# Squares' products between the next operand's products, the state's copy taken from PSUM, nine merge tiles, and an earlier reordering of the past

## The chip, the core and the metric

The kernel runs on one core of one Trainium2 chip. That core has a matrix engine (TensorE, PE in the profile, with its weight loads as PEld), a vector engine (VectorE, DVE), a scalar engine (ScalarE, ACT), a general engine (GpSimd, POOL), and a sync engine (SP) that here issues most of the transfers between the chip's memory (HBM, "dram" in names) and the core's two memories: SBUF, which holds operands, and PSUM, into which TensorE adds its products. PSUM is used here as eight banks, named pa, pb, pc, pd, pe, mm, mf and so on after the tags of their tiles. The metric is the device time of one execution, in microseconds (us), as the median of several runs.

## The reference

One layer of a hybrid encoder. A normalised input h of 1152 rows (1024 of a prompt, and 8 x 16 of samples) by 1024 is multiplied by one combined matrix; its columns feed three things: forgetting attention ("fox", 8 heads of 64), a gated delta rule ("gdn", 8 heads of 64), and two gates.

```python
h   = RMSNorm_pre(x)
z   = h @ W_in          # fox q,k,v,forget logits | gdn qkv,a,b,out-gate | merge gates A,B
yA  = P_fox(FoX(h))     # exp-decayed causal attention, prompt and sample with a cached past
yB  = P_gdn(GDN(h))     # short causal conv, l2-normalised q and k, gated DeltaNet
x  += RMSNorm_post(W_out(sigmoid(gA)*yA + sigmoid(gB)*yB))
x  += RMSNorm_post(W_down relu(W_up RMSNorm_pre(x))^2)
```

For this change two pieces matter. `l2norm` divides each row of q and k by the root of the sum of its 64 squares. And the delta rule walks over the rows in chunks of 64 with a 64 x 64 state per head:

```python
v_new = u - w @ state
o     = (q * exp(gc)) @ state + ((q @ k.T) * decay) @ v_new
state = state * exp(g_last) + (k * exp(g_last - gc)).T @ v_new
```

## The kernel before

Every large product runs in three passes of 32-bit operands that were split into a rounded part and a rest (hi x hi, lo x hi, hi x lo): `mm3` (L158) issues them, so nearly every big product of the profile has line 158. In the front half each is 128 x 128 weights against 384 columns, a third of the 1152 rows ("a chunk", c = 0, 1, 2); one operand of 128 columns takes 8 x 3 = 24 of them for each chunk. "The big products" below are these.

The program has these stages, by time in the profiled execution: norm, transposes and logits to about 60 us; the delta rule to about 700; fox attention to about 977; the merge of the two with their gates to about 1110; then the output projection and the two MLP products to the end.

**The delta rule's stage** works on four pairs of heads, p = 0 to 3. For a pair, `gdn_in` makes three operands (q, k, v; i = 0, 1, 2) with `gemm_t` into the banks mm, copies them out of PSUM (`ev`), and passes each through the short convolution. For q and k `gdn_squares` squares the operand on ScalarE (L455) and adds the squares over a head's 64 rows by nine small products of 128 x 128 against two columns of ones (L457; each appears as two passes in the trace, so 18 for one operand, 144 in all), into one bank pa; VectorE scales them (L458). `gdn_norms` turns the result into rows in HBM (transposition L660, then stores), and `gdn_systems` fetches these rows back spread over the partitions and multiplies k by them on GpSimd (L482), q on VectorE, and so on, to the small products L520. An inverse of each chunk's triangle follows, then the chain over the chunks. It is this chain that walks with the state S: for each chunk u and pair of heads, L619 multiplies by the state, L620 (VectorE) makes the right side R, L621 multiplies it by the inverse, L623 takes vn out of PSUM, L626 makes the update, L629 makes the new state S on VectorE out of the old one and the PSUM bank, and L633 makes the output out of qa and xs; xs holds a copy of the state in its lower half (L618, one head on VectorE and one on ScalarE, each 64 x 64) and vn in its upper half (L625).

**Fills.** Big products that nothing waits for soon (fox's q, k, v and the merge's gates; tile mf, spilled to HBM through gst) are issued at a low priority, and the scheduler, which writes out one order for each engine from a model of durations when the program is built, lays them where it expects TensorE to wait. There are 2232 of them. They run out at some point, and where, the scheduler decides.

**Fox** begins with the cached past's forget values (`fox_past`, L951 to L953): two GpSimd copies put the columns in another order (q, b, h in place of b, q, h), and a transposition follows. **The merge** loads the outputs of both halves from HBM (`load`, L1167, tiles orw of 128 x 384), splits them, and multiplies for each of eight j by the two projections' weights (raw_..._w_proj_fox and raw_..._w_proj_gdn, split into whi and wlo); the result times the gate goes into a tile mt (L1192), and the sum of both is split into mhi and mlo, which take the place of hhi and hlo in SBUF, the operands of the fills. orw and mt share seven buffers of one tag; two more (wor) receive rows of W_out.

SP issues its transfers strictly in the order written out, so one that waits holds up all behind it; the same holds of every engine's instructions.

## Time and profile before

| | |
|---|---|
| median of 3 runs | 1936.88 us (1934.66 to 1941.57) |
| the profiled execution | 1936.41 us, span 1934.7 us |
| TensorE busy | 1869.5 us, 97% |
| VectorE, ScalarE, GpSimd busy | 1281.3, 996.8, 231.3 us |
| mean granted TensorE clock | 0.987 |
| squares' products L457 | 144, at 74.2 to 465.5 us |
| state's copy L618 on VectorE | 60, at 228.2 to 657.9 us |

The span runs from the first to the last instruction; the 1.7 us beside it lie around the program. A matmul's busy time overlaps its successor's, so what a product costs TensorE is the distance between two starts, not its duration. Idle time "before" an instruction is put down to the instruction that released it. The granted clock is 1 at full speed; a stretch with about 0.5 is one in which TensorE ran at half of it.

### The profile page before, as it was taken

How to read it: one execution, taken by the hardware profiler on the slowest of the kernel's cores; microseconds unless marked ns; L12 is line 12 of the kernel's file. 1: busy time of each engine (PE TensorE's matmuls, PEld its weight loads, DVE VectorE, ACT ScalarE, POOL GpSimd, SP SyncE). 2: the span in 40 equal slices, each digit the busy share in tenths (PEclk: the TensorE clock that was granted, in tenths of full speed). 3: DMA queues.
4: the chain of work that ended last, by engine and by line, in shares of the span. 5: the costliest groups of instructions: out<-in, count | busy, mean ns of one | idle time of the engine just before them, and what ended most of it. 6: DMA issues, size and time to landing. Idle time of an engine off the chain costs nothing. (4 is left out here: it accounts for less than half of the span.)

```text
span 1934.7 us, 31970 instructions
## 1 busy us (share of the span) xinstructions
PE 1869.5 (97%) x11036; PEld 1695.0 (88%) x11036; DVE 1281.3 (66%) x3077; ACT 996.8 (52%) x2373; POOL 231.3 (12%) x348
## 2 busy tenths in 40 slices
PE   7999999999999999999999999999999999999998
PEld 6989989889889888787889988999999998888886
DVE  7457487587664457766654455886667764559697
ACT  6433374474564666666554444555544554345553
POOL 2141332331521110000002200000000000000000
PEclk9989998999999999999999999999999999999999
DMA  7142413323335264434264462234444469846573
GB/s 217 38 104 66 114 43 99 95 68 90 89 85 162 81 192 142 131 113 121 67 211 136 130 210 93 59 115 138 131 137 135 143 188 298 281 150 182 149 263 135
DMA packets 292693, 261.35 MB, mean 135 GB/s; under 512 B 68742, under 2 KB 246910, under 8 KB 292531
## 3 DMA queue, kind: packets, MB, share of 16 engines
q1 hardware_dynamic: 252486, 225.10, 39.5%
q10 hardware_dynamic: 40044, 34.21, 5.4%
q8 instruction: 87, 1.43, 0.3%
q14 instruction: 76, 0.61, 0.1%
HBM read 186.48 MB, written 72.75 MB: 134 GB/s over the span
## 5 line engine op out<-in xcount | busy, mean ns | idle before, releaser
L158 PE MATMUL mf<-hhi,whi 128*128 128x384 f32 x744 | 262.2, 352 | 1.8 <-ACT gst L219 1.8
L158 PE MATMUL mf<-hlo,whi 128*128 128x384 f32 x744 | 262.3, 353 | 0.0
L158 PE MATMUL mf<-hhi,wlo 128*128 128x384 f32 x744 | 261.2, 351 | 0.0
L158 PE MATMUL mm<-th,wh 128*128 128x320 f32 (+1 forms) x896 | 177.9, 294 | 0.0
L158 PE MATMUL mm<-bh,ah 128*128 128x512 f32 x436 | 169.7, 389 | 0.7 <-DVE y L1633 0.7
L158 PE MATMUL mm<-bh,al 128*128 128x512 f32 x436 | 169.7, 389 | 0.0
L158 PE MATMUL mm<-bl,ah 128*128 128x512 f32 x436 | 169.6, 389 | 0.0
L334 ACT CAST ah<-ar 128x512 fp32r<-128x512 f32 x107 | 66.4, 622 | 153.8 <-PE mm L158 102.2
L158 PEld LDWEIGHTS mf<-hhi,whi 128*128 128x128 f32 x744 | 141.5, 190 | 3.1 <-ACT gst L219 2.3
L158 PEld LDWEIGHTS mm<-th,wh 128*128 128x128 f32 x896 | 143.5, 188 | 0.0
L158 PEld LDWEIGHTS mf<-hhi,wlo 128*128 128x128 f32 x744 | 141.7, 191 | 0.3
L158 PEld LDWEIGHTS mf<-hlo,whi 128*128 128x128 f32 x744 | 141.3, 190 | 0.5
L158 PE MATMUL mm<-th,wl 128*128 128x256 f32 x448 | 132.2, 295 | 0.0
L1397 DVE TENSOR_TENSOR s<-mm,s 128x256 f32<-128x256 f32 (+1 forms) x196 | 84.4, 454 | 65.7 <-PE mm L158 53.9
L335 DVE TENSOR_TENSOR al<-ar,ah 128x512 fp32r<-128x512 f32 x107 | 73.6, 689 | 73.8 <-ACT ah L334 73.0
L335 DVE TENSOR_TENSOR wlo<-raw,whi 128x512 fp32r<-128x512 f32 x110 | 78.2, 715 | 65.3 <-ACT whi L334 63.7
L158 PE MATMUL mm<-hhi,whi 128*128 128x384 f32 x288 | 106.5, 370 | 1.6 <-ACT X L395 1.6
L334 ACT CAST whi<-raw 128x512 fp32r<-128x512 f32 x110 | 67.7, 620 | 67.5 <-PE mf L158 28.8
L158 PE MATMUL mm<-hhi,wlo 128*128 128x384 f32 x288 | 102.4, 356 | 0.0
L158 PE MATMUL mm<-hlo,whi 128*128 128x384 f32 x288 | 102.3, 355 | 0.0
L158 PE MATMUL mm<-mhi,wl 128*128 128x256 f32 (+1 forms) x336 | 99.1, 295 | 0.0
L158 PE MATMUL mm<-mhi,wh 128*128 128x256 f32 (+1 forms) x336 | 98.8, 294 | 0.0
(542 smaller groups left out, 4951.9 us busy)
## 6 DMA issues: line engine op xcount, KB each, us to landing
ar<-ua_d SPq DMA_DIRECT2D x124, 256.0 KB
raw<-in_w_in_dram SPq DMA_DIRECT2D x86, 256.0 KB
br<-in_w_down_dram SPq DMA_DIRECT2D x78, 256.0 KB
wr<-in_w_up_dram SPq DMA_DIRECT2D x56, 256.0 KB
ua_d<-s SPq DMA_DIRECT2D x112, 128.0 KB
ua_d<-s ACTq DMA_DIRECT2D x84, 128.0 KB
gate_d<-gst ACTq DMA_DIRECT2D x48, 192.0 KB
ga<-gate_d SPq DMA_DIRECT2D x48, 192.0 KB
```

The source lines that it names most:

```text
L158: T.matmul(out, a, b, start=first and i == 0, stop=last and i == n - 1)
L334: A.copy(h, raw)
L335: V.tensor_tensor(l, raw, f(h), ALU.subtract)
L1397: V.tensor_tensor(r, o, x, ALU.add)
```

## The change

Four edits. **Squares:** `gdn_squares` yields after each of its nine products; `gdn_in` hands the generator to the next operand's `gemm_t`, which, in its last chunk (c = 2), takes one square's product after every three big ones, and what is left at the end. **State's copy:** VectorE's half of xs is no longer copied from S, but made by the same operation as S, from the old state and the PSUM bank, as a 64 x 64 piece (`state`); ScalarE's half is copied from S as before. **Merge tiles:** orw and mt have nine buffers, wor has one. **Past:** the columns are put in order by GpSimd at p = 2 of the delta rule's stage, into a tile of its own, clq.

```diff
--- before.py
+++ after.py
@@ -155,7 +155,8 @@
     def mm3(out, pairs, first=True, last=True):
         n = len(pairs)
         for i, (a, b) in enumerate(pairs):
-            T.matmul(out, a, b, start=first and i == 0, stop=last and i == n - 1)
+            mm = T.matmul(out, a, b, start=first and i == 0, stop=last and i == n - 1)
+        return mm
 
 
     phs = ctx.enter_context(ExitStack())
@@ -348,21 +349,28 @@
                 lo += [l[:, i] for i in range(4)]
         return hi, lo
 
-    def gemm_t(w, xhi, xlo, kt, evac, tag=("mm", 1), prio=1):
+    def gemm_t(w, xhi, xlo, kt, evac, tag=("mm", 1), prio=1, between=iter(())):
 
         whi, wlo = w
         for c in range(3):
             cs = slice(c * CH, (c + 1) * CH)
             acc = pt(*tag)
-            mm3(acc[:, :CH], [pr for k in range(kt) for pr in (
-                (whi[k], tk(xhi, k, c)), (whi[k], tk(xlo, k, c)), (wlo[k], tk(xhi, k, c)))])
+            for k in range(kt):
+                mm = mm3(acc[:, :CH], [(whi[k], tk(xhi, k, c)), (whi[k], tk(xlo, k, c)), (wlo[k], tk(xhi, k, c))],
+                         k == 0, k == kt - 1)
+                if c == 2:
+                    with tc.issue_after(mm.ins):
+                        next(between, None)
             with tc.high_priority(prio):
                 evac(c, acc[:, :CH])
+        for _ in between:
+            pass
 
 
     fox_d = dr.tile([NP_, P, NT], F32, name="fox_d")
     gdn_d = dr.tile([NP_, P, NT], F32, name="gdn_d")
     cl = cb.tile([P, 2, 64], F32, name="cl")
+    clq = cb.tile([P, P], F32, name="clq")
     ngc = cb.tile([P, 1], F32, name="ngc")
     for h in range(2):
         S.dma_start(ngc[64 * h:64 * h + 64], gdn_norm_g[0].unsqueeze(1))
@@ -384,6 +392,7 @@
 
         xt = []
         nv = big(gp, "nv", 2, [P, 3, 36])
+        sq = iter(())
         for i in range(3):
             x = big(gp, "X", XB, [P, XW])
             xv = x[:, 3 + NPR:].rearrange("p (b t) -> p b t", b=NB)
@@ -397,10 +406,10 @@
                     A.copy(x[:, 3 + 2 * CH:3 + NPR], acc[:, 0:256])
                     A.copy(xv[:, :, 3:19], acc[:, 256:384].rearrange("p (b t) -> p b t", b=NB))
             gemm_t(weights(halves(win, W_G + 512 * i + p * P), "w", HI),
-                   hhi, hlo, KT, ev)
+                   hhi, hlo, KT, ev, between=sq)
             xt.append(gdn_conv(gp, p, i, x))
             if i < 2:
-                gdn_squares(gp, i, xt[i], nv)
+                sq = gdn_squares(gp, i, xt[i], nv)
             next(lg, None)
         return *xt, nv
 
@@ -455,6 +464,7 @@
         A.activation(sq, a, AF.Square)
         for t in range(NTT):
             T.matmul(nps[:, t:t + NTT + 1:NTT], sq[:, t * P:(t + 1) * P], ones2, start=True, stop=True)
+            yield
         V.tensor_scalar(nv[:, 0, 2 * NTT * j:2 * NTT * (j + 1)], nps[:, :2 * NTT], 0.25, 0.25 * EPS, ALU.mult, ALU.add)
 
     def gdn_norms(gp, p, qs, ks, vs, nv):
@@ -614,8 +624,8 @@
                     rr = R[:, i]
                     xs = big(gp, "xs", 2, [P, 2, C])
                     if u:
-                        for h in range(2):
-                            (A.copy if h else V.tensor_copy)(xs[0:64, h], st_[64 * h:64 * h + 64])
+                        state(xs[0:64, 0], 0, 64)
+                        A.copy(xs[0:64, 1], st_[64:128])
                         T.matmul(pu[:, 0:C], kbd[:, i], st_, start=True, stop=True)
                         V.scalar_tensor_tensor(rr, pu[:, 0:C], cols[:, 3, u:u + 1], rr, ALU.mult, ALU.subtract)
                     T.matmul(pu[:, C:2 * C], ybd[:, i], rr, start=True, stop=True)
@@ -625,10 +635,14 @@
                         A.copy(xs[64:128, h], vn[64 * h:64 * h + 64])
                     T.matmul(pu[:, 2 * C:3 * C], kd[:, i], vn, start=True, stop=True)
                     st0, st_ = st_, big(gp, "S", 2, [P, C])
-                    if u:
-                        V.scalar_tensor_tensor(st_, st0, gam[:, u:u + 1], pu[:, 2 * C:3 * C], ALU.mult, ALU.add)
-                    else:
-                        V.tensor_copy(st_, pu[:, 2 * C:3 * C])
+
+                    def state(dst, r0, r1, st0=st0, pu=pu, u=u):
+
+                        if u:
+                            V.scalar_tensor_tensor(dst, st0[r0:r1], gam[r0:r1, u:u + 1], pu[r0:r1, 2 * C:3 * C], ALU.mult, ALU.add)
+                        else:
+                            V.tensor_copy(dst, pu[r0:r1, 2 * C:3 * C])
+                    state(st_, 0, P)
                     k0 = 0 if u else 64
                     T.matmul(po[:, i * P:(i + 1) * P], xs[k0:].rearrange("p h c -> p (h c)"),
                              qa[k0:, u].rearrange("p h c -> p (h c)"), start=True, stop=True)
@@ -925,6 +939,10 @@
                 lf_out(gp)
             if p == 2:
                 conv_out(gp)
+
+                for k in range(2):
+                    G.tensor_copy(clq[:, 64 * k:64 * k + 64].rearrange("p (q b h) -> p q b h", q=NP_, b=NB),
+                                  cl[:, k].rearrange("p (b q h) -> p q b h", b=NB, q=NP_))
             if p == 1:
                 for k in range(2):
                     S.dma_start(cl[:, k].rearrange("p (b h) -> p b h", b=NB),
@@ -945,12 +963,7 @@
     def fox_past(fp):
 
         ct = mmt()
-        cq = fp.tile([P, 4 * P], F32, tag="sp3", name=nm("past"))[:, :P]
-
-        for k in range(2):
-            G.tensor_copy(cq[:, 64 * k:64 * k + 64].rearrange("p (q b h) -> p q b h", q=NP_, b=NB),
-                          cl[:, k].rearrange("p (b q h) -> p q b h", b=NB, q=NP_))
-        T.transpose(ct[:, 0:P], cq, ident)
+        T.transpose(ct[:, 0:P], clq, ident)
         fl, on = (fp.tile([P, n * P], F32, tag=f"sp{n - 1}", name=nm("past"))[:64, :PAST + TS] for n in (6, 7))
         G.memset(on, 1.0)
         V.tensor_copy(fl[:, 0:P], ct[0:64, 0:P])
@@ -1163,7 +1176,7 @@
         olo = op.tile([P, 8, NT], F32R, name="olo")
         def load(k, c):
             cs = slice(c * CH, (c + 1) * CH)
-            orw = op.tile([P, CH], F32, tag="mt", bufs=7, name=nm("orw"))
+            orw = op.tile([P, CH], F32, tag="mt", bufs=9, name=nm("orw"))
             S.dma_start(orw, fox_d[k, :, cs] if k < 4 else gdn_d[k - 4, :, cs])
             split(orw, ohi[:, k, cs], olo[:, k, cs])
 
@@ -1174,14 +1187,14 @@
                         load(k, c)
         for j in range(KT):
             if j == 4:
-                w2 = [wo_part(oqa, 0, 0, WK, oqa, "wor", 2)]
+                w2 = [wo_part(oqa, 0, 0, WK, oqa, "wor", 1)]
             js = slice(j * P, (j + 1) * P)
             whi, wlo = weights([w_pf[0][:, js], w_pg[0][:, js]], "w", 200)
             mt = {}
 
             for c, i in [(c, i) for i in (1, 0) for c in range(3)] if j == 0 else [(c, i) for c in range(3) for i in (1, 0)]:
                 cs = slice(c * CH, (c + 1) * CH)
-                mt[c, i] = op.tile([P, CH], F32, tag="mt", bufs=7, name=nm("mt"))
+                mt[c, i] = op.tile([P, CH], F32, tag="mt", bufs=9, name=nm("mt"))
                 ga = op.tile([P, CH], F32, tag="ga", bufs=GAB, name=nm("ga"))
                 with tc.high_priority(200):
                     S.dma_start(ga, gate_d[i, j, :, cs])
```

The first place is TensorE in the delta rule's stage, the first pair, where the squares of q lay in one piece between products of the next operand (mm). Before:

```order
L158 MATMUL mm_3775<-hhi,whi_3739 128x384
L158 MATMUL mm_3775<-hlo,whi_3739 128x384
L158 MATMUL mm_3775<-hhi,wlo_3740 128x384
L457 MATMUL pa_3698<-ones_534,y_3699 128x2 x9
L158 MATMUL mm_3775<-hhi,whi_3739 128x384
L158 MATMUL mm_3775<-hlo,whi_3739 128x384
L158 MATMUL mm_3775<-hhi,wlo_3740 128x384
```

Now, in that operand's last chunk (mm_3789 is its bank):

```order
L158 MATMUL mm_3789<-hhi,whi_3727 128x384
L158 MATMUL mm_3789<-hlo,whi_3727 128x384
L158 MATMUL mm_3789<-hhi,wlo_3728 128x384
L466 MATMUL pa_3793<-ones_534,y_3794 128x2
L158 MATMUL mm_3789<-hhi,whi_3727 128x384
L158 MATMUL mm_3789<-hlo,whi_3727 128x384
L158 MATMUL mm_3789<-hhi,wlo_3728 128x384
L466 MATMUL pa_3793<-ones_534,y_3794 128x2
```

The nine small products (18 passes) no longer follow each other: there are three big ones between each of them, and the last two stand together at the chunk's end, about 42 big products later than the piece stood.

The second place is VectorE in the first steps of the chain. Before, the copy of S follows the operation that made S:

```order
L623 TENSOR_SCALAR vn_4926<-pb_4919 128x64
L643 TENSOR_SCALAR nv_3587<-pd_4899 128x2
L629 SCALAR_TENSOR_TENSOR S_4931<-S_4892,gam_4088,pb_4919 128x64
L618 COPY xs_4935<-S_4931 64x64
L490 TENSOR_TENSOR y_4720<-ks_4429,y_4699 128x576
L620 SCALAR_TENSOR_TENSOR R_4907<-pd_4934,cols_4064,R_4907 128x64
L490 TENSOR_TENSOR y_4720<-ks_4429,y_4699 128x576
L623 TENSOR_SCALAR vn_4941<-pd_4934 128x64
```

Now:

```order
L633 TENSOR_SCALAR vn_4927<-pb_4920 128x64
L500 TENSOR_TENSOR y_4721<-ks_4430,y_4700 128x576
L642 SCALAR_TENSOR_TENSOR S_4932<-S_4893,gam_4089,pb_4920 128x64
L642 SCALAR_TENSOR_TENSOR xs_4936<-S_4893,gam_4089,pb_4920 64x64
L500 TENSOR_TENSOR y_4721<-ks_4430,y_4700 128x576
L630 SCALAR_TENSOR_TENSOR R_4908<-pd_4935,cols_4065,R_4908 128x64
L496 TENSOR_TENSOR qs_4307<-qs_4307,y_4716 128x576
L633 TENSOR_SCALAR vn_4942<-pd_4935 128x64
L611 TENSOR_SCALAR kd_608<-pe_5013,tm 64x64
L496 TENSOR_TENSOR qs_4307<-qs_4307,y_4716 128x576
```

The copy has become a second operation on the PSUM bank (pd, pb); the chain's own operations stand in the same order, and those of the next systems (L490, now L500, and L487, now L496) are still laid between them.

The third place is TensorE after fox's last value product (L1035, now L1048). Before, 79 fills stand behind it, then the merge's first products, with single fills (mf) among them:

```order
L158 MATMUL mf_3531<-hlo,whi_3493 128x384
L158 MATMUL mf_3531<-hhi,wlo_3494 128x384
L158 MATMUL mf_3531<-hhi,whi_3499 128x384
L158 MATMUL pb_11337<-ohi,whi_11329 128x384
L158 MATMUL pb_11337<-olo,whi_11329 128x384
L158 MATMUL pc_11355<-ohi,whi_11329 128x384
L158 MATMUL pc_11355<-olo,whi_11329 128x384
L158 MATMUL mf_3531<-hlo,whi_3499 128x384
L158 MATMUL pb_11337<-ohi,wlo_11330 128x384
L158 MATMUL pb_11337<-ohi,whi_11329 128x384
```

Now 30 fills stand behind it, and then the merge begins, with fox's half (whi_11323):

```order
L158 MATMUL mf_3560<-hhi,whi_3500 128x384
L158 MATMUL mf_3560<-hlo,whi_3500 128x384
L158 MATMUL mf_3560<-hhi,wlo_3501 128x384
L158 MATMUL pe_11391<-ohi,whi_11323 128x384
L158 MATMUL pe_11391<-olo,whi_11323 128x384
L158 MATMUL pe_11391<-ohi,wlo_11324 128x384
```

The other 84 of the 114 fills that stood behind fox's last product (the last 34 of them behind some 220 merge products) now stand earlier, most of them in the delta rule's stage. On SP, at the same place, the second weight of the merge now follows the last of the 24 loads; before it stood behind the eighth:

```order
L1167 DMA orw_11249<-gdn_d 128x384
L1167 DMA orw_11253<-gdn_d 128x384
L343 DMA raw_11327<-in_w_proj_gdn_dram 128x4x128
L1167 DMA orw_11257<-gdn_d 128x384
L1167 DMA orw_11261<-gdn_d 128x384
```

```order
L1180 DMA orw_11309<-fox_d 128x384
L1180 DMA orw_11313<-fox_d 128x384
L1180 DMA orw_11317<-fox_d 128x384
L344 DMA raw_11327<-in_w_proj_gdn_dram 128x4x128
L1200 DMA ga_11352<-gate_d 128x384
```

The load of the weight raw_11327 has moved past 16 loads of orw.

## The prediction

> **What bounds the kernel now.** I read the page first, then the clock in windows, then TensorE's waits.
>
> ```profile
> PE 1869.5 (97%) x11036; PEld 1695.0 (88%) x11036; DVE 1281.3 (66%) x3077; ACT 996.8 (52%) x2373; POOL 231.3 (12%) x348
> ```
>
> TensorE is busy for 97% of the span, and no other engine is near it. So only three things shorten the run: fewer passes (the change keeps every big product), waits of TensorE, and stretches in which its clock is granted at half. Next, the windows around the stretches in which the page's row of the granted clock falls (the columns are start and end, length, PE busy and instructions, granted clock, DMA share, GB/s):
>
> ```profile
> 91.40:94.80 3.40, 3.40 (x29) 1.00 0.02 5
> 94.80:101.70 6.90, 6.90 (x27) 0.51 0.15 38
> 296.20:299.60 3.40, 3.40 (x29) 1.00 0.03 7
> 299.60:306.50 6.90, 6.90 (x26) 0.51 0.17 38
> 323.50:326.90 3.40, 2.49 (x19) 1.00 0.54 146
> 326.90:333.80 6.90, 6.90 (x25) 0.51 0.36 118
> 463.50:466.90 3.40, 3.32 (x25) 1.00 0.33 58
> 466.90:470.30 3.40, 3.40 (x12) 0.50 0.31 73
> 1040.30:1047.20 6.90, 5.05 (x16) 0.51 0.62 193
> ```
>
> TensorE is busy in these stretches and slow. The timeline shows what that costs, one big product after the other, and what stood ahead:
>
> ```profile
> 463.58 2.17 PE L457 MATMUL pa<-ones,y 128*128 128x2 f32 x18 [0.77 <-ACT y L455]
> ...
> 466.38 0.34 PE L158 MATMUL mm<-hhi,whi 128*128 128x384 f32 x1
> 466.56 0.34 PE L158 MATMUL mm<-hlo,whi 128*128 128x384 f32 x1
> ...
> 467.22 0.52 PE L158 MATMUL mm<-hlo,whi 128*128 128x384 f32 x1
> 467.54 0.52 PE L158 MATMUL mm<-hhi,wlo 128*128 128x384 f32 x1
> ```
>
> Big products start 0.175 us apart at full clock and 0.32 apart at half, so a half-clock stretch loses 1 - 0.175/0.32 = 45% of its length: 3.1 us for 6.9, 1.5 for 3.4. Last, the waits (engine, tile and line, releaser, total us, times, longest):
>
> ```profile
> PE pb L621 <- DVE R L620: 5.8, 7, 1.6
> PE pd L621 <- DVE R L620: 4.8, 6, 1.6
> PE pe L158 <- DVE mt L1192: 4.2, 1, 4.2
> PE pa L1000 <- DVE m L1004: 2.1, 1, 2.1
> PE mm L953 <- POOL past L951: 0.7, 1, 0.7
> ```
>
> **Squares.** The same windows for L457 alone show where the pieces lie (busy time of its products, then of their weight loads; of the four windows, those with the least and the most):
>
> ```profile
> 323.50:326.90 3.40, 1.33 (x13) 1.42 (x13) 1.00 0.54 146
> 463.50:466.90 3.40, 2.17 (x18) 2.08 (x18) 1.00 0.33 58
> ```
>
> In each of the four windows that end where a half-clock stretch begins, TensorE spends 1.3 to 2.2 of 3.4 us on products with two columns. Two of these windows have no idle time at all. I read this as: the clock is granted by how many columns were streamed, and the squares stream almost none. With three big products between two of them, the mix of the last chunk is 3 x 0.175 us of full work for each pair of passes of 0.226 (18 passes in 463.58 to 465.61 are 0.113 each), so 70% full: no window falls low on their account. Removed: 6.9 + 6.9 + 6.9 + 3.4 = 24.1 us at half clock, x 45% = 10.9 us. Also removed: the waits ahead of the squares, 0.8 us in the timeline above, and in the window from 323.5 the idle 3.40 - 2.49 = 0.9 us, because ScalarE's squares are now made two chunks of products ahead. Together **-12.6 us**.
>
> The passes themselves cost the same wherever they stand, if an isolated pair costs what one in a piece does. The nearest row is another product of that shape, also a pair of passes between others:
>
> ```profile
> 234.65 0.41 PE L642 MATMUL pd<-ones,osq 128*128 128x2 f32 x2
> 234.92 0.67 PE L158 MATMUL mm<-hhi,whi 128*128 128x384 f32 x1
> ```
>
> The pair at 234.65 holds TensorE for 0.27 us, against 0.226. For 72 pairs that is 0 to 72 x 0.044 = 3.2 us; that pair's successor was already in a slow window, so I take 0 and keep 3 for the range.
>
> What is late next: the sum of squares is complete 42 big products (7.3 us) later, and so are the norms (L660), their rows, and GpSimd's multiplication of k by them (L482), behind which the small products L520 and L592 of that pair are queued on TensorE.
>
> ```profile
> L660 PE MATMUL pa<-ident,nv x4: 271/272/277, 107.7 to 474.9; 128*36 128x128 f32 x4
> L482 POOL TENSOR_TENSOR ks<-ks,y x4: 2632/2648/2677, 118.1 to 504.1; 128x1152 f32<-128x1152 f32 x4
> 118.11 2.68 POOL L482 TENSOR_TENSOR ks<-ks,y 128x1152 f32<-128x1152 f32 x1 [1.17 <-DMA y<-rows_n]
> ```
>
> From L660 to L482 the first pair takes 118.1 - 107.7 = 10.4 us, waiting for the rows' transfer; the last takes 504.1 - 474.9 = 29.2, held by other work, so there 19 us of slack cover the 7.3, and the two between lie alike. For the first pair there is no slack: k is ready 13.1 us after L660 (118.11 + 2.68 - 107.70), and between L660 and the first product that needs it the order now has 59 big products (10.3 us) in place of 79. That leaves 13.1 - 10.3 = **+2.8 us** of new wait; bounds 0 (the fills' places differ) and 7.3.
>
> **State's copy.** Sixty copies on VectorE:
>
> ```profile
> L618 DVE COPY xs<-S x60: 177/187/2105, 228.2 to 657.9; 64x64 f32<-64x64 f32 x60
> 231.39 2.63 POOL L482 TENSOR_TENSOR ks<-ks,y 128x1152 f32<-128x1152 f32 x1
> 231.97 2.10 DVE L618 COPY xs<-S 64x64 f32<-64x64 f32 x1
> 234.41 0.41 PE L621 MATMUL pb<-R,ybd 128*128 128x64 f32 x2 [1.60 <-DVE R L620]
> L629 DVE SCALAR_TENSOR_TENSOR S<-S,gam,pd x32: 263/281/282, 231.3 to 660.2; 128x64 f32<-128x64 f32 x32
> ```
>
> The median copy is 187 ns, the longest 2105; the one at 231.97 runs to 234.07 and ends with GpSimd's L482 (231.39 + 2.63 = 234.02), and R stands behind it, and TensorE behind R for 1.60 us. L629, which reads PSUM and runs in the same stretches, stays between 263 and 282 ns. So the new operation should take about 0.28 us and not stretch. Of TensorE's 5.8 + 4.8 = 10.6 us of waits for R in the whole run, the window from 366 to 386, where the third pair's L482 runs beside the chain, holds these:
>
> ```profile
> PE pb L621 <- DVE R L620: 2.1, 2, 1.6
> PE pd L621 <- DVE R L620: 1.8, 2, 1.6
> ```
>
> Four waits, two of 1.6, which is the size of a long copy less a short one. With the one at 234.41 that makes 5.5 us that I put down to copies, and the remaining 5.1 us in small waits in part; against it stands the longer plain operation (+0.1 us for each copy where VectorE is late). I take **-6 us**, and -1.5 for the half-clock stretch that begins at 234.8, right after the wait of 1.60. Bounds: 0, if another operation of VectorE is then stretched in the copy's place (L490 and L496 lie in the same queue), and -10.6, all waits of both rows.
>
> **Past.** The two GpSimd copies leave fox's start: -0.7 us for the wait at L953 at most. The next wait, L1000 for m (2.1 us), hangs on a transfer that the change leaves alone, so part of the 0.7 is only passed on: **-0.3**.
>
> **The merge.** The order has 30 fills behind fox's last value product (976.47 us) in place of 79, and none among the merge's first products.
>
> ```profile
> 976.50:990.30 13.80, 13.80 (x81) 1.00 0.74 218
> 990.30:1008.00 17.70, 14.66 (x82) 1.00 0.97 311
> L334 ACT CAST ohi<-orw x24: 498/513/516, 981.3 to 1002.0; 128x384 fp32r<-128x384 f32 x24
> 994.26 0.51 ACT L334 CAST ohi<-orw 128x384 fp32r<-128x384 f32 x1 [0.25 <-DMA orw<-fox_d]
> 986.24 0.43 SPq L343 DMA_DIRECT2D raw<-in_w_proj_gdn_dram  x1
> 988.02 1.92 SPq L1167 DMA_DIRECT2D orw<-gdn_d  x4
> ```
>
> Before, TensorE works through to 990.3, then waits 17.70 - 14.66 = 3.0 us up to 1008, 4.2 for mt up to 1042 (mhi takes the place of hhi, which the last fill must have read), and loses 45% of 6.9 = 3.1 at half clock: 10.3 in all. After, 30 fills last 5.2 us, to 981.7 on the same scale. Fox's first cast came at 994.3; it loses the weight's issue and gap ahead of it (986.24 to 988.02, 1.8 us) and its cast, so about 992. TensorE idles 10.3 us; then 24 fox products (4.2 us) run, and gdn's weight, now issued behind all 24 loads, is split at about 998.5 to 999.5, another 2 to 3 us. After so long a pause I count one or two half-clock windows, 1.5 to 3.1. In all 14 to 16.5; the wait for mt is gone, since the fills have ended. The balance is **+5 us**; bounds -1 (nine buffers bring the loads 6 us earlier) and +9 (gdn's weight 4 us later).
>
> **The sum**, on the profiled execution's 1936.41: -12.6 + 2.8 - 7.5 - 0.3 + 5 = -12.6, so 1923.8; that run is 0.47 below the median, so **1924.3 us** stands against 1936.88.
>
> **Rivals.** First, the half-clock stretches do not come from the squares. For it: four other pieces of the same squares are followed by none, and the window at 323.5 also holds 0.9 us of waiting. Against it: two of the four have no idle time. Then 10.9 us stay, and the result is 1935, no change. [...]
>
> Second, VectorE's waits stay: the copy no longer stretches, but the operations beside it in the queue do, and R is as late as before; the sum loses 7.5 us: 1932, at the edge of what can be told. [...]
>
> Third, slower: the norms' chain takes over. If L482 of the second to fourth pairs follows L660 as closely as the first pair's does, because the systems' other work no longer holds it, each of four pairs waits up to 7.3 us and is followed by a half-clock stretch of 1.5: 35 in place of 2.8, so 1956. It turns slower than now (by 6 us) from about 5.4 us per pair. Against it stand the 19 us of slack.
>
> **How the numbers follow.** This kernel can tell about 0.3% (5.8 us) from no change: faster means below 1931.1. Chances: the forecast 0.70, with its own range 1916 to 1931 (the merge's bounds and the norms' wait give -6 to +5); the first rival 0.11; the second 0.12; the third 0.07. The forecast is faster in nearly all of its range; the second rival in half, the first hardly: 0.70 + 0.06 + 0.01 = 0.77 faster; 0.17 the same; 0.06 slower. The range that leaves two in ten out takes in the first rival: 1913 to 1935.
>
> **What would show it.** Right: the granted clock stays 1 behind the squares; the xs operation stays within 0.26 to 0.30 us while L482 runs; between 982 and 999 (less what was gained before) TensorE is idle for over 10 us; no wait for mt at the fills' end; a wait of about 3 us at the first pair's L592 or L520. Wrong: half-clock stretches behind the last chunks, L620 still late while GpSimd works, or waits behind L482 of the second pair.

## The result, and the profile after

The changed kernel takes 1914.18 us (median of 6 runs, 1906.80 to 1915.69) against 1936.61 us before: a ratio of 0.9879 with a 95% interval of 0.9858 to 0.9900, or 22.4 us less where 12.6 were forecast. It lies inside the range of 1913 to 1935 by 1.2 us, and below the forecast's own range of 1916 to 1931. Its profiled execution, 1906.80 us, is the fastest of the six, so a second profile of the same kernel was taken in the experiments (1914.09 us); the table below has both.

The page of the changed kernel:

```profile
span 1905.1 us, 31985 instructions
PE 1849.2 (97%) x11036; PEld 1679.0 (88%) x11036; DVE 1271.0 (67%) x3077; ACT 998.7 (52%) x2373; POOL 236.3 (12%) x348
```

TensorE issues the same 11036 passes, and is the bound as before. To see where time went, I added up for each stage how much later than at full clock and without a wait each pass was followed by the next (0.174 us for 384 columns, 0.227 for 512, 0.146 for 320, 0.119 for 256, 0.112 for 128 and fewer; a shorter distance counts as a gain). This is worked out from all of TensorE's rows in the traces; the last two columns are of the first two experiments below:

```
us lost by TensorE            before   after  after again  squares  state's copy
                             1936.41  1906.80    1914.09     alone     alone
start to 60 us                   8.6     8.3        8.8       8.9       8.4
first pair, up to its chain     15.7    11.2       13.0      11.9      11.6
first chain, up to the second   23.4    13.3       15.5      15.2      17.9
second chain, up to the third   18.7    13.2       13.4      15.1      20.4
third chain, up to the fourth   14.2    11.8       11.4      16.0      11.3
fourth chain                     5.8     5.1        5.0       5.3       5.4
up to fox's first value          7.2     4.4        3.7       6.2       6.3
fox                             32.9    27.5       28.3      35.3      31.9
merge                           10.5    16.0       17.2      10.2      14.3
rest                             3.6     0.3        1.9       5.1       3.4
sum                            140.6   111.1      118.2     129.2     130.9
at half clock, 60 us to merge   41.0     6.8       13.7      13.7      27.3
```

The sums differ as the profiled times do: 140.6 - 111.1 = 29.5 us, and 1936.41 - 1906.80 = 29.6. The delta rule's stage gives most, the merge takes some back, and fox, for which next to nothing was forecast, gives about 5. In the second profile of the same kernel the sum is 22.4 us lower than before, which is the difference of the medians; the 7 us between the two profiles are taken up below.

TensorE's waits in the changed kernel, the rows that answer to those shown before (L530, L602, L631 and L1013 are the old L520, L592, L621 and L1000):

```profile
PE pe L158 <- ACT ohi L335: 10.5, 1, 10.5
PE pa L530 <- ACT kqt L527: 2.8, 2, 2.6
PE pa L1013 <- DVE m L1017: 1.5, 1, 1.5
PE pb L631 <- DVE R L630: 1.4, 1, 1.4
PE pe L602 <- ACT kd L613: 0.9, 2, 0.7
```

The waits for R have gone from 10.6 us to 1.4; the wait for mt (4.2) has gone; one of 10.5 us stands at the merge's beginning. The last row is to be read beside this one of the kernel before, which stands at 134.8 us:

```profile
PE pe L592 <- ACT kd L603: 4.6, 1, 4.6
```

The windows around the only two half-clock stretches left between 60 us and the merge:

```profile
130.40:133.80 3.40, 0.87 (x5) 1.00 0.00 0
133.80:137.20 3.40, 3.15 (x12) 0.50 0.07 28
505.90:509.30 3.40, 1.68 (x13) 1.00 0.00 0
509.30:512.70 3.40, 3.40 (x16) 0.50 0.00 0
```

Both follow a window in which TensorE was idle for half of the time or more, at L530 and in the chain; the squares' products, at 78.5 to 84.0, 100.1 to 105.5 and so on to 451.7 to 457.2, are followed by none.

VectorE, before (L490 and L486, the multiplications by rows that the section on the change calls L490 and L487, and L496, the other operation that the prediction names beside L490) and after (the xs operation L642, and L500, L496 and L506, the same three; L496 is another operation in each kernel):

```profile
L490 DVE TENSOR_TENSOR y<-ks,y x8: 740/758/1176, 120.8 to 507.6; 128x576 f32<-128x576 f32 x8
L486 DVE TENSOR_TENSOR qs<-qs,y x8: 741/754/2127, 123.9 to 511.9; 128x576 f32<-128x576 f32 x8
L496 DVE TENSOR_TENSOR y<-y,madd x8: 674/692/1774, 128.7 to 514.9; 128x512 f32<-128x512 f32 x8
```

```profile
L642 DVE SCALAR_TENSOR_TENSOR xs<-S,gam,pd x28: 262/267/269, 228.9 to 646.4; 64x64 f32<-64x64 f32 x28
L642 DVE SCALAR_TENSOR_TENSOR xs<-S,gam,pb x28: 263/265/268, 232.6 to 649.7; 64x64 f32<-64x64 f32 x28
L500 DVE TENSOR_TENSOR y<-ks,y x8: 759/952/1287, 122.0 to 497.4; 128x576 f32<-128x576 f32 x8
L496 DVE TENSOR_TENSOR qs<-qs,y x8: 744/1034/2591, 126.0 to 499.7; 128x576 f32<-128x576 f32 x8
L506 DVE TENSOR_TENSOR y<-y,madd x8: 675/721/1207, 130.1 to 503.9; 128x512 f32<-128x512 f32 x8
```

None of the 56 xs operations L642 leaves 262 to 269 ns, where the copy reached 2105. The big multiplications beside it have become longer, 952 and 1034 ns at the median for 758 and 754; L506 with 721 for 692 hardly has.

The merge's beginning, in windows from fox's last value product on:

```profile
958.90:964.20 5.30, 5.30 (x33) 1.00 0.50 91
964.20:974.80 10.60, 0.57 (x4) 0.78 0.98 327
974.80:992.00 17.20, 16.25 (x77) 0.84 0.84 273
```

The 30 fills last 5.3 us, TensorE then idles for 10.0, and the first products run partly at half clock.

### The profile page after: what moved, and what is told of

Same layout as the page of the kernel before. It is cut to its first block, busy times and chain, and to the rows that moved or that the text cites. A ratio compares the mean times of both kernels' runs of the same rounds, so it can differ in the third digit from the quotient of the medians.

```text
span 1905.1 us, 31985 instructions
## 1 busy us (share of the span) xinstructions
PE 1849.2 (97%) x11036; PEld 1679.0 (88%) x11036; DVE 1271.0 (67%) x3077; ACT 998.7 (52%) x2373; POOL 236.3 (12%) x348
## 3 DMA queue, kind: packets, MB, share of 16 engines
q8 instruction: 87, 1.43, 0.3%
## 4 chain that ended last, share of the span: by engine, by line
PE 75%; ACT 4%; DVE 3%; DMA 3%; issue 1%; POOL 1%; SPq 0%; ACTq 0%; DVEq 0%; POOLq 0%
PE mm L158 45%; PE mf L158 13%; PE pc L1048 2%; PE pb L1039 1%; PE pc L647 1%; PE mm L1077 1%; PE pd L1039 1%; PE mm L1098 1%; PE pa L158 1%; PE pc L158 1%; PE pd L158 1%; PE pb L158 1%; PE pe L158 1%; DMA qv<-fr_d 1%; PE pa L530 1%
## 5 line engine op out<-in xcount | busy, mean ns | idle before, releaser
L158 PE MATMUL mm<-mlo,wh 128*128 128x256 f32 (+1 forms) x336 | 98.6, 293 | 0.0
```

The source lines that it names most:

```text
L158: mm = T.matmul(out, a, b, start=first and i == 0, stop=last and i == n - 1)
```

## The experiments

Ratios are to the kernel before on the same chip. "The changed kernel" is 0.9879 (0.9858 to 0.9900) in the first measurement.

**The squares alone.** The kernel before with the hunks of the diff for `mm3`, `gemm_t`, `gdn_in` and `gdn_squares`, and nothing else.

```diff
-                gdn_squares(gp, i, xt[i], nv)
+                sq = gdn_squares(gp, i, xt[i], nv)
```

> The kernel before with the squares' edit alone: nine products of squares laid between the next operand's big products, everything else as before. Theory on record: the half-clock stretches that followed the four pieces of squares (24.1 us) are gone, and with them the 1.7 us of waits ahead of the squares; the first pair's norms come later and cost up to 2.8 us. That is -9.8 us: about 1927. Rival (the half-clock stretches have another cause and come back within a few us of where they were): -1.7 + 2.8, so 1936 to 1938, with as much half-clock time in the delta rule's stage as before. The fills behind fox's last value product are 114 as before, so the merge should cost what it did (10.3 us of waits and half clock).

Measured: 1923.04 us, ratio 0.9918 (0.9894 to 0.9942), so 11 to 21 us less. Between 60 us and the merge 13.7 us are left at half clock of 41.0, none behind the squares. Its waits show what this edit does not touch and what it adds (L630 is L621, L529 is L520):

```profile
PE pb L630 <- DVE R L629: 6.4, 7, 1.6
PE pd L630 <- DVE R L629: 2.0, 3, 1.0
PE pa L529 <- ACT kqt L526: 3.0, 1, 3.0
```

R is late by 8.4 us, with the copies as they were. The first pair's norms cost a wait of 3.0 us at 135.5. It stands where the 4.6 us at L592 (kd) stood before, of which 0.9 are left: the new wait has taken the old one's place and is not added to it.

The big multiplications on VectorE (L499 and L495 here) are long in this run already, in which the copy was not touched:

```profile
L499 DVE TENSOR_TENSOR y<-ks,y x8: 739/1058/1291, 123.2 to 491.2; 128x576 f32<-128x576 f32 x8
L495 DVE TENSOR_TENSOR qs<-qs,y x8: 739/1017/2672, 127.2 to 495.6; 128x576 f32<-128x576 f32 x8
```

**The state's copy alone.** The kernel before with the two hunks in the chain.

```diff
-                            (A.copy if h else V.tensor_copy)(xs[0:64, h], st_[64 * h:64 * h + 64])
+                        state(xs[0:64, 0], 0, 64)
+                        A.copy(xs[0:64, 1], st_[64:128])
```

> The kernel before with the state's copy made from PSUM, alone. Theory on record: no xs operation on VectorE is stretched beside GpSimd, TensorE's waits for R (10.6 us) fall by about 6, and the half-clock stretch after 234.8 us (1.5) goes: -7.5. In this order 47 fills stand behind fox's last value product in place of 114, the rest having moved ahead, so the merge begins with a wait of about 4 us but has no wait for mt at its end: -7.5 and about -2 there, so 1927 to 1929. Rival (other operations of VectorE are stretched in the copy's place and R stays late): waits for R of 8 us or more, and 1934 to 1937.

Measured: 1928.16 us, ratio 0.9950 (0.9931 to 0.9969), 6 to 13 us less. From its waits:

```profile
PE pd L621 <- DVE R L620: 0.9, 1, 0.9
PE pb L158 <- ACT whi L334: 6.9, 1, 6.9
PE pe L592 <- ACT kd L603: 4.9, 3, 4.5
```

R's waits fall from 10.6 us to 0.9, the kd wait stays, and a wait of 6.9 us appears at the merge. The sum came out as expected, but by luck: 9.7 us came off the waits for R in place of 6, the merge became 3.8 us dearer and not 2 cheaper, and the first pair lost 4.1 us less (11.6 for 15.7), which the expectation did not have. There the squares stand in one piece as before, but the half-clock stretch of 6.8 us behind the second piece did not come; three of the eight pieces were followed by half clock, where in the kernel before it was four. In the written order 47 fills are left behind fox with this edit alone, 114 with the squares alone, and 30 with both: it is the state's copy that uses up the fills earlier.

**Nine tiles alone.**

```diff
-            orw = op.tile([P, CH], F32, tag="mt", bufs=7, name=nm("orw"))
+            orw = op.tile([P, CH], F32, tag="mt", bufs=9, name=nm("orw"))
...
-                w2 = [wo_part(oqa, 0, 0, WK, oqa, "wor", 2)]
+                w2 = [wo_part(oqa, 0, 0, WK, oqa, "wor", 1)]
```

> The kernel before with nine buffers for orw and mt and one for wor, alone. The written order then begins the merge with fox's half in place of gdn's, and puts 24 of the last fills between the merge's first products. Theory: the tiles are what turned the merge's beginning round; the fills still cover most of it, and the wait for mt (4.2 us) becomes shorter because only 6 fills are left to wait for: -4 to +3 us, so 1933 to 1940. Rival (nine tiles let the loads run ahead and shorten the merge's beginning): fox's first product before 990 on this run's scale, and 1930 or less.

Measured: 1937.89 us, ratio 1.0001 (0.9981 to 1.0020). No difference. The merge begins with fox's half and waits at its start, and the wait for mt did not become shorter as I expected:

```profile
PE pd L158 <- DVE mt L1192: 5.0, 1, 5.0
PE pe L158 <- ACT ohi L334: 2.2, 1, 2.2
```

This run also has each operand's squares in one piece. Five of its eight pieces were followed by half clock, against four in the kernel before, with the same order on TensorE in that stage.

**The changed kernel with seven tiles.**

```diff
-            orw = op.tile([P, CH], F32, tag="mt", bufs=9, name=nm("orw"))
+            orw = op.tile([P, CH], F32, tag="mt", bufs=7, name=nm("orw"))
```

(and mt and wor in the same way)

> The changed kernel with seven buffers for orw and mt and two for wor as before, and the other three edits. The merge then begins with gdn's half, with 30 fills behind fox's last value product as in the changed kernel. Theory: the changed kernel's wait of 10.5 us at the merge comes from beginning with fox's half, whose loads are the last of 24; with gdn's half first the wait is 5 us or less and the time 5 to 6 us below the changed kernel's, about 1908 against 1936.6 before. Rival (the wait comes only from the fills having run out): a wait of about 9 to 11 us here too, and the changed kernel's time, 1912 to 1916.

Measured: 1914.06 us, ratio 0.9879 (0.9855 to 0.9902): the changed kernel's. The merge begins with gdn's half and waits for its weight:

```profile
PE pb L158 <- ACT whi L335: 8.0, 1, 8.0
```

It loses 16.2 us in that stage, as with nine tiles. The rival holds: with the fills gone, which half comes first makes no difference here, where something that it needs is issued late either way.

**The squares in one piece, without a wait.** The changed kernel without the lines that put a square's product between big ones; the nine follow each other, and the scheduler placed them behind ScalarE's squares.

```diff
-                if c == 2:
-                    with tc.issue_after(mm.ins):
-                        next(between, None)
```

> The changed kernel with each operand's nine products of squares in one piece again, placed behind ScalarE's squares so that TensorE need not wait for them; the other edits as changed. Theory (the clock is granted by what was streamed, and a piece of squares streams next to nothing): half-clock stretches follow 3 to 6 of the eight pieces, 10 to 30 us at half clock in the delta rule's stage against 3 to 7 in the changed kernel, and the time is 5 to 12 us above the changed kernel's: 1919 to 1926. Rival (the waits ahead of the squares made the half clock, not the squares): no stretch follows a piece, and 1912 to 1916.

Measured: 1928.48 us, ratio 0.9969 (0.9952 to 0.9985). None of the eight pieces was followed by half clock. So a piece of squares does not always do it, and the cause as I had put it is not enough. The time is high all the same, above both ranges that were given, for waits of another place, the first pair's (L599 is L592):

```profile
PE pe L599 <- ACT kd L610: 5.2, 1, 5.2
PE pe L599 <- POOL ks L489: 2.8, 1, 2.8
```

and for 32.9 us lost in fox, where the order is another one than in the changed kernel. The run settles less than it seems: the traces' stretches of half clock last 3.41, 6.83 or 10.24 us, and in the traces of the kernel before and of the changed one they begin whole steps of 3.413 us apart (277 steps from 94.83 to 1040.33 us, 245 from 133.81 to 970.08). I take these steps as the clock's windows and lay their borders out over each run's whole trace, and by these borders only two of the eight pieces lie whole in one window; most of the others are split between two.

What then stood beside the pieces in the kernel before? TensorE's groups in one of the two windows without idle time, 296.2 to 299.6 (17 of the piece's 18 passes lie in it):

```profile
L457 PE MATMUL pa<-ones,y 128*128 128x2 f32 x17 | 2.0, 251 | 0.0
L158 PE MATMUL mm<-hhi,wlo 128*128 128x384 f32 x2 | 0.9, 471 | 0.0
L724 PE MATMUL pc<-qa,be 128*128 128x32 f32 x6 | 0.8, 274 | 0.0
L721 PE MATMUL pd<-be,kd 128*128 128x256 f32 x2 | 0.6, 377 | 0.0
L158 PE MATMUL mm<-hlo,whi 128*128 128x384 f32 x1 | 0.3, 335 | 0.0
L158 PE MATMUL mm<-hhi,whi 128*128 128x384 f32 x1 | 0.3, 332 | 0.0
```

Six passes with 32 columns (L724) stand in the same window, so only four big ones of 384 are left. In the window from 91.4 it was L822 and L823 (64 and 8 columns), in that from 323.5 a wait of 0.9 us; in that from 463.5 there was next to nothing, 0.1 us of idle time. The mended theory: what decides is the share of the full clock's columns that is streamed in one window of 3.41 us. The full clock is estimated at 2.4 columns per ns here, from 256 more columns taking 0.227 - 0.119 = 0.108 us, so a full window has about 8190. By this estimate a piece of 2.0 us alone leaves a share of about 0.38, which mostly passed (of the windows with 0.35 to 0.40, counted at the end of this document, 2 of 87 were followed by half clock), and anything short or idle beside it in the same window takes the share lower (below 0.30, 69 of 71 were followed).

The run with nine tiles alone has a piece that shows how near the edge 0.38 is. At 184.3 us one lies whole in a window with nine products of 384 columns and nothing else, no wait and no short product (a share of 0.37), and half clock follows:

```profile
184.20:187.60 3.40, 3.40 (x27) 1.00 0.58 182
187.60:191.00 3.40, 3.40 (x13) 0.50 0.00 0
```

So a piece did it alone here, as one of the 2 in those 87.

**One big product between two squares.** The changed kernel, with a square's product behind each of the three passes of the first three k in place of one behind each k.

```diff
-                mm = mm3(acc[:, :CH], [(whi[k], tk(xhi, k, c)), (whi[k], tk(xlo, k, c)), (wlo[k], tk(xhi, k, c))],
-                         k == 0, k == kt - 1)
+                for n, pr in enumerate([(whi[k], tk(xhi, k, c)), (whi[k], tk(xlo, k, c)), (wlo[k], tk(xhi, k, c))]):
+                    mm = mm3(acc[:, :CH], [pr], k == 0 and n == 0, k == kt - 1 and n == 2)
...
```

> The changed kernel with one big product between two squares' products in place of three, so the nine fill a third of the last chunk: 0.175 us of full streaming for each 0.226 us of squares, 44% over some 3.6 us. Theory: this lies above the share (about a third) at which half-clock stretches began in the kernel before, so hardly any stretch follows: one or none, and 1912 to 1917. Rival (the share that decides lies higher, near a half): stretches behind two or more of the eight, and 1917 to 1922.

Measured: 1916.62 us, ratio 0.9912 (0.9893 to 0.9932). No half clock follows any of the eight: one big product for each pair, 44% of the time and a share of 0.41 of the columns in the lowest window, was enough here.

**The pieces at the chunk's end, single and doubled.** The changed kernel, with the nine products right behind the last big product of the chunk; then the same with each of them issued twice (the second writes the same numbers over the first).

```diff
-                if c == 2:
+                if c == 2 and k == kt - 1:
                     with tc.issue_after(mm.ins):
-                        next(between, None)
+                        for _ in between:
+                            pass
```

and, for the doubled ones, this line ahead of the same one:

```diff
+            T.matmul(nps[:, t:t + NTT + 1:NTT], sq[:, t * P:(t + 1) * P], ones2, start=True, stop=True)
```

> The changed kernel with each operand's nine products of squares in one piece right behind the last big product of that chunk, where the changed kernel ends them too; ScalarE's squares are long done there. Theory, as mended by the run with the pieces put early (none of its eight pieces was followed by half clock): a half-clock stretch follows a window of 3.41 us in which less than about a third of the full clock's columns were streamed; a piece of 2.0 us that is followed and preceded by big products leaves about 0.38 and passes, unless something else in the same window is short too. So at most two of the eight pieces are followed by half clock, and the time differs from the changed kernel's (about 1914) only by what the written order does elsewhere (61 fills behind fox, -3 to +12 us). Theory as it stood on record (the piece alone is enough): four or more of eight.

> As the run with the pieces at the chunk's end, but every product of squares is issued twice in succession (the second overwrites the first with the same numbers), so a piece is 36 passes, 4.1 us. Mended theory: of the windows that a piece of 4.1 us covers, one is filled by 2 to 3.4 us of it, leaving a share of 0 to 0.4, so half-clock stretches of 1.5 to 3.1 us lost follow five or more of the eight pieces; with 8 x 2.03 = 16 us of passes that makes 24 to 38 us above the run with single pieces, about 1940 to 1955. Rival (squares never set the clock): no stretch behind the pieces, 16 us above, about 1932 to 1936.

Measured: single 1917.62 us, ratio 0.9911 (0.9886 to 0.9936); doubled 1942.01 us, ratio 1.0051 (1.0031 to 1.0072). Windows with a single piece and those behind them:

```profile
104.00:107.40 3.40, 3.40 (x28) 1.00 0.81 169
107.40:110.80 3.40, 3.40 (x21) 1.00 0.47 135
462.40:465.80 3.40, 3.40 (x28) 1.00 0.00 0
465.80:469.20 3.40, 3.40 (x21) 1.00 0.00 0
```

and with a doubled one:

```profile
83.50:86.90 3.40, 3.40 (x31) 1.00 0.00 0
86.90:90.30 3.40, 3.40 (x13) 0.51 0.33 82
482.90:486.30 3.40, 3.40 (x31) 1.00 0.00 0
486.30:489.70 3.40, 3.40 (x12) 0.50 0.00 0
```

TensorE is busy in all of these. None of the eight single pieces is followed by half clock (three of them lie whole in one window), and all eight doubled ones are. The doubled run takes 24.4 us more than the single one, at the lower end of what was expected; but the two differ in the written order elsewhere (30 fills behind fox's last value product, and 61 with single pieces). The changed kernel has 30 too, and took 1911.25 us beside them. Against it the doubled pieces cost 30.8 us: 8 x 2.03 = 16.2 for the passes, 8 x 1.55 = 12.4 for eight stretches of 3.4 us, and 2 more.

**The merge's weights first.** The changed kernel, with the first j's two weights ahead of the loads and gdn's ahead of fox's.

```diff
+        w0g, w0f = weights([w_pg[0][:, :P]], "w", 210), weights([w_pf[0][:, :P]], "w", 200)
         for k0 in (4, 0):
...
-            whi, wlo = weights([w_pf[0][:, js], w_pg[0][:, js]], "w", 200)
+            whi, wlo = weights([w_pf[0][:, js], w_pg[0][:, js]], "w", 200) if j else (w0f[0] + w0g[0], w0f[1] + w0g[1])
```

> The changed kernel with the merge's first two weights issued ahead of the loads, gdn's first, and gdn's half of the merge first; nine buffers, 30 fills behind fox's last value product. Theory: the changed kernel's 10.5 us and the 8.0 us of the run with seven buffers both end with what was issued last on SP of what the first product needs (fox's loads there, gdn's weight here); with gdn's weight and loads issued first, the wait is 2 to 4 us and the merge's start follows the loads: 6 to 8 us below the changed kernel, about 1907. Rival (the loads' and casts' pace decides, whatever comes first): the idle time moves behind the first products and sums up to 9 us or more, and 1912 to 1916.

Measured: 1906.57 us, ratio 0.9867 (0.9847 to 0.9888). The waits at the merge:

```profile
PE pd L158 <- ACT whi L335: 3.3, 2, 2.3
PE pb L158 <- ACT ohi L335: 2.9, 2, 2.1
```

are 6.2 us, more than the 2 to 4 expected, where the changed kernel had 10.5 and some small ones; the stage loses 12.2 us in place of 16.0 and 17.2. The gain of 4 to 5 us in the stage is shown by the profiles; as a time it can't be told from the changed kernel, whose interval overlaps.

**A part of the fills kept back.** That kernel, with the last 72 fills held on TensorE until fox's last value product.

```diff
-            for w0, dst in todo[NE:]:
+            for w0, dst in todo[NE:-1]:
...
         values(*late)
+        with tc.issue_after(lastmm[0].ins):
+            with tc.high_priority(-LOW):
+                for w0, dst in todo[-1:]:
+                    spill(w0, dst, "f", "mf", 20, MFB)
```

> The kernel with the merge's first weights issued ahead (gdn's first), with the last item of the fills (72 products, 12.6 us) kept back on TensorE until fox's last value product. Theory: the merge's remaining idle time (about 6 us of waits and 3 us lost at half clock) is covered by fills that the earlier stages do not miss: 3 to 8 us below 1906.6, so 1899 to 1904. Rival (the 42 fills taken out of the stages before leave waits there of the same size): the merge's waits go and as much comes back before it, 1904 to 1909.

Measured: 1911.44 us, ratio 0.9884 (0.9858 to 0.9910), above both expected ranges and the same as the changed kernel beside it (1911.25). The merge now loses only 6.3 us for 12.2, but fox loses 35.9 in place of 28.2, and nearly 7 of these 7.7 us in its last third, which has 100 fills in place of 139. The rival holds: the fills had been covering waits there.

**Without the past's edit.** The changed kernel with the two GpSimd copies at fox's beginning again.

```diff
-        T.transpose(ct[:, 0:P], clq, ident)
+        cq = fp.tile([P, 4 * P], F32, tag="sp3", name=nm("past"))[:, :P]
+        for k in range(2):
+            G.tensor_copy(cq[:, 64 * k:64 * k + 64].rearrange("p (q b h) -> p q b h", q=NP_, b=NB),
...
```

> The changed kernel without the past's edit: GpSimd's two copies stand at the beginning of fox again; the other three edits stay. Theory on record: 0.3 us, so the changed kernel's time, 1912 to 1916, and fox's stage loses what it does in the changed kernel (27.5 us against the ideal spacing, where the kernel before loses 32.9). Rival (fox's 5 us came from the past's edit): 1917 to 1920, with fox's stage back at some 33 us lost.

Measured: 1917.07 us, ratio 0.9915 (0.9894 to 0.9935). A wait of 0.5 us for the copies is back at the transposition (L966), but the way to fox's first value loses 4.4 us as in the changed kernel, so in sum the copies cost nothing there. But fox loses 31.4 us in place of 27.5 and 28.3, with its fills at other places (163, 164 and 145 in its thirds; with the edit 157, 174 and 139). The times point the same way, 0.9915 against 0.9879 and 0.9880, but the intervals overlap. That the other order of the fills is the cause is argued from the counts and was not tried by itself.

**The changed kernel again**, beside the last three.

> The changed kernel once more, beside the three others on the same chip. Theory: 1912 to 1916, the same stages' losses as in its first profile within 2 us each, and the granted clock at 1 behind all eight operands' squares. If its first profiled execution (7 us below its median) was an exception, this profile shows which stage that was.

Measured: 1911.25 us (1907.91 to 1914.09), ratio 0.9880 (0.9856 to 0.9905). Its profiled execution is the slowest of its six and lies 7.3 us above the first profile. Its half-clock time up to 1060 us is 27.3 us against 17.1, which at 45% is 4.6 of the 7.3; a stretch at 323.2 us, behind a window with a wait ahead of the next operand, and longer ones at 135.5 and 971.7 make it. The order is the same, only the windows lie otherwise. Behind the squares the clock stays at 1 in all eight places here too.

Taken together: the squares alone and the state's copy alone give 0.8% and 0.5%, and all four edits 1.2%. So the first two account for the gain, and neither the tiles nor the past have an effect on the time that these runs can tell.

## Why the prediction was right, and where its sizes were off

The terms point the right way and the main mechanisms are shown, but 22.4 us against 12.6 is more than the forecast's own range allowed; that the time still lies in the wider one, by 1.2 us, is luck.

**Squares, -12.6 us.** Right in what goes and about in size: with this edit alone all of the stretches behind the pieces are gone, 27.3 us less at half clock where 24.1 were worked out, and 11 to 21 us less in time. Which pieces are followed differs between executions, though (four of eight before, five with the same order and nine tiles), so 24.1 us was the size of one execution. Too simple was the step "the squares stream almost none": a piece by itself lies at the edge. None of the 16 single pieces of the two runs with pieces was followed by half clock, most of them split between two windows; one with nine tiles was, with nothing but big products beside it. Three of the four in the kernel before had company in the window. The first rival is answered by this too: the half clock did depend on the squares, together with the wait of 0.9 us that it named and with the short products beside them. One part of the term was misread. The 0.9 us of idle time in the window from 323.5 is not a wait for the squares but one for X, the copy of the chunk before out of the bank mm, and such a wait still stands ahead of that operand in the changed kernel; the first line is before, the second after:

```profile
324.41 0.44 PE L158 MATMUL mm<-hhi,whi 128*128 128x384 f32 x1 [1.20 <-ACT X L395]
318.77 0.45 PE L158 MATMUL mm<-hhi,whi 128*128 128x384 f32 x1 [1.82 <-ACT X L404]
```

For half clock no idle time was needed: windows busy for 3.40 of 3.40 us were followed by half clock, those from 91.4 and 296.2 in the kernel before and those from 83.5, 107.4, 179.1 and 482.9 in the doubled run.

**The first pair's wait, +2.8 us.** The wait came, 2.6 us in its place (L530) and 3.0 with the squares alone. As a term of the sum it was mis-sized: the old wait of 4.6 us at L592 was taken to stay, and has shrunk to 0.9 in the first profile (2.5 in the second), because the new wait took its place. In balance 0.9 us less, or 0.7 more, in place of 2.8 more.

**State's copy, -6 and -1.5.** The mechanism is right, the size too small: waits for R went from 10.6 us to 1.4 (to 0.9 with this edit alone), so -9.2. In the kernel before, 12 of the 13 waits in those two rows have a copy L618 of 0.6 us or more among VectorE's operations of the 3.2 us before them, and these 12 make 9.2 us: nearly all of it was the copies', where I had put most of the small waits down to something else. Of the two waits of 1.6 us in the window from 366 that I read as long copies, though, only the one at 376.1 has a copy of 2105 ns ahead; the other, at 371.8, has one of 706 ns. The thirteenth, 1.43 us at 520.1, stands behind other long operations (L497, 1.53 us), and so does the one of 1.4 us that the changed kernel keeps, at 239.7 (L506, 1.20 us). The second rival is seen in that one place, and not in the rest: VectorE's big multiplications became longer (952 and 1034 ns for 758 and 754), yet no other wait for R is left. But they did not become longer in the copy's place: with the squares alone, where the copies stay, they take 1058 and 1017 ns. Why they do is open. That they have slack in the queue, while the copy stood straight between the state and R, is my reading, argued and not tried.

**Past, -0.3.** The wait of 0.7 us at L953 is gone, but as a term nothing is to be seen of it: the way to fox's first value loses the same 4.4 us with the copies and without. Whether the edit does something to fox is the term below.

**The merge, +5.** Measured 16.0 and 17.2 us for 10.5, so +5.5 and +6.7: 10.5 us of idle time where 10.3 were worked out, and 10.2 or 13.7 us at half clock where one or two stretches of 3.4 were counted. The reason given was half right: the fills having run out is the cause (with the state's copy alone a wait of 6.9 us is there too, and with the fills kept back the stage loses 6.3 us for 12.2), while beginning with fox's half costs nothing of its own, as the seven tiles showed.

**What the sum left out: fox, -5.** Fox's stage was taken as it was. It lost 32.9 us before and 27.5 and 28.3 after, without an edit inside it. Most of the edits make the scheduler write another order there; of the variants, those with the changed kernel's fills in fox's thirds (about 157, 174 and 139) lose 27.5 to 28.4 us, the others 31 to 36. That the fills' places cause it is argued from these counts and was not tried by itself. Together the mis-sized terms are 3 us for R, 2 to 4 for the first pair and 5 for fox, less 0.5 to 1.7 for the merge, about the 10 us between forecast and result. Profile by profile the account does not close quite: in the second, 22.3 us below the kernel before, 1.5 us stay open, and in the first, 29.6 us below, about 5, of which 3 are half-clock time (34.1 us less at half clock, where 24.1 and 3.4 were worked out).

**The third rival** did not come: no wait stands behind L482 of the second to fourth pairs, and the chains' stages lose less than before.

## What to carry to other kernels

Where a matrix engine is nearly always busy, look at the granted clock in windows as long as its shortest stretch (3.41 us here), and count the columns streamed in them rather than the idle time: here short products cost a second time when enough of them fell into one window (all eight doubled pieces were followed by half clock), and laying them between long ones removed that (none of eight). A copy from SBUF to SBUF on VectorE took up to 2105 ns for 187 while GpSimd worked; where its value can be made from PSUM, try that: here it took 262 to 269 ns, also in the 23 of 56 operations that ran beside one of GpSimd's. And where a scheduler fills waits with spare work, an edit that removes waits also moves that work: ask where the fills run out, because the stage that had them last pays, and here taking them back only moved the bill.

## What the runs showed of the hardware that was not expected

How closely the granted clock followed the streamed columns. Over all fourteen profiles (60 to 1100 us), for windows of 3.41 us at full clock, I worked out the share of the full clock's columns (2.4 per ns, as above) that TensorE streamed in them, and counted those followed by half clock:

```
share of columns    windows    followed by half clock
below 0.30               71        69
0.30 to 0.35             35        10
0.35 to 0.40             87         2
0.40 and above         3950         0
```

Idle time alone is not what decided here: among windows in which TensorE was busy for 99% or more, all 10 below 0.30 were followed by half clock, 3 of the 43 from 0.30 to 0.40, and none of the 3024 above. Between 0.30 and 0.40 the share alone did not tell (12 of 122 were followed); what does is open. And the windows lay differently in two executions of the same order: a border lies at 133.8 us in the first profile of the changed kernel and at 135.5 in the second, half a window apart. The two had 17.1 and 27.3 us at half clock, which at 45% is 4.6 of the 7.3 us between them.
